# A decoder layer's last LayerNorm: square root on ScalarE with the reciprocal on VectorE, two and a half blocks scaled by TensorE, one store from ScalarE's queue

## The chip, the cores and the metric

The kernel runs on one core of one Trainium2 chip. The time is device microseconds of one execution; lower is better. The program is fully unrolled: there are no loops at run time, and each of the five engines (TensorE, VectorE, ScalarE, GpSimd, SyncE; PE, DVE, ACT, POOL, SP in the profile) works through its own list of instructions in order and waits on semaphores that the other engines and the transfers raise.

## The reference

One layer of a hybrid decoder on 256 tokens of width 2048 in float32: a feed-forward network (SwiGLU) with a residual and a LayerNorm, a mixer of sparse attention and a recurrent branch with its residual and LayerNorm, and a second SwiGLU with residual and LayerNorm. The change concerns only the last statement, and in it only what is done once the sums are there:

```python
def layer_norm(x, g, b):
    mu = jnp.mean(x, axis=-1, keepdims=True)
    var = jnp.mean(jnp.square(x - mu), axis=-1, keepdims=True)
    return (x - mu) * lax.rsqrt(var + LN_EPS) * g + b
...
h = layer_norm(DN_ALPHA * h + 0.5 * swiglu(h, ffn2_w_in, ffn2_w_out), ln3_g, ln3_b)
```

## The kernel before

All large products run on TensorE, float32 split into a high and a low part, so that a product is three matmuls (lines 732 to 734). The 256 tokens are two groups of 128, one token to a partition: t = 0 and t = 1. The 2048 columns are four blocks of 512: nb = 0 to 3. `Y[t][nb]` is a tile of 128 x 512 in SBUF that holds the residual, and in the end the output.

The end of the program is `out_product` of the second feed-forward network. `last_blocks` finishes the products in such an order that both blocks 2 and 3 of group 0 are done first, then block 2 of group 1, and last block 3 of group 1 in two halves of 256 columns (line 1064 adds a half to the residual, line 1065 takes its statistics; 877 and 878 do that for a whole block). Group 0 is normalised while TensorE still works on group 1. `OuterNorm.finish` then normalises group 1; nothing else is left to do in the program, so this is where it ends.

The norm of a group goes in these steps. `chain(t)` turns the statistics into mean and variance (`bn_aggr`, line 887), adds epsilon (888), and raises that to the power -1/2 on GpSimd (889); `self.mv[t]` is the mean and `self.r[t]` the reciprocal root. `first(t, nb)` is one VectorE instruction that subtracts the mean and multiplies by the gain row (996). `second(t, nb)` is another one that multiplies by `self.r[t]` and adds the bias row (1000), and after it `leave` issues the store of the block (1004).

For some blocks of group 1 the second step goes another way: TensorE has beforehand put the bias row into a PSUM tile, as identity times row (992); ScalarE makes a diagonal matrix `diag` out of the identity and `self.r[1]` (1011, tile `dg`); `by_pe` lets TensorE add `diag` times the block to the PSUM tile (1015), and ScalarE copies the result back to SBUF (1016). Before the change that is block 0 whole and block 1 in two halves of 256. Blocks 2 and 3 of group 1 go through VectorE, and VectorE takes the blocks in the order 2, 0, 1, 3.

A scheduler orders the instructions by the order of the code, with some pulled forward (`tc.high_priority()`). All nine stores are issued by SyncE, in the order in which `leave` is called. `SM`, `BP` and `U` hand out small tiles, PSUM tiles and 128 x 512 tiles; `T`, `V`, `A` and `G` are TensorE, VectorE, ScalarE and GpSimd; `S` is 256 and `P` 128.

Of the kernel before, what the change touches and what calls it, by code (L numbers as in the profile page):

```python
# [11 lines left out]
AF = mybir.ActivationFunctionType  # L12
# [3 lines left out]
P = 128  # L16
S = 256
# [11 lines left out]
EPS = 1e-5  # L29
# [331 lines left out]
def tile_layer(ctx, tc, x_fm, x_tm, pos, f1a, f1o, wA, wki, wB, wG, lru, wab, wrb, wo, f2a, f2o,  # L361
               cols_d, ln1_g, ln1_b, ln2_g, ln2_b, ln3_g, ln3_b, out):
    nc = tc.nc
# [4 lines left out]
    V, A, T, G = nc.vector, nc.scalar, nc.tensor, nc.gpsimd  # L368
    count = [0]

    def name(s):
        count[0] += 1
        return f"{s}{count[0]}"

    def U(s="u", dt=F32):
        return pool.tile([P, 512], dt, name=name(s), tag="u", bufs=U_BUFS)
# [7 lines left out]
    def SM(n, s="s", dt=F32):  # L384
        return pool.tile([P, 32], dt, name=name(s), tag="sm", bufs=21)[:, :n]

    def C(shape, s, dt=F32):
        return pool.tile(shape, dt, name=s)

    def MM():  # L390
        return psum.tile([P, 512], F32, name=name("mm"), tag="mm", bufs=4)

    def BP():
        return psum.tile([P, 512], F32, name=name("bp"), tag="bp", bufs=4)
# [60 lines left out]
    for i in range(NR + LAG):  # L455
# [4 lines left out]
        if i >= LAG:  # L460
            g, c = divmod(i - LAG, TPG)
            o = sum(LRU_COLS[:c])
# [62 lines left out]
        G.memset(invf[:, i:i + 1], float(THETA ** (-(2.0 * i) / 32)))  # L525
    mhalf = C([P, 1], "mhalf")
    G.memset(mhalf, -0.5)

    def col(k, i):
        o, w = COLS[k]  # L530
        return cols[:, o + i:o + i + 1]

    ident = C([P, P], "ident")
# [141 lines left out]
    Y = [[None] * 4 for _ in range(2)]  # L675

    sums = [[[spill.tile([P, 512], F32, name=name("ya")) for _ in range(4)] for _ in range(2)] for _ in range(2)]
# [149 lines left out]
    def blockA(x, finish=None, lag=0, ln=None):  # L827
# [18 lines left out]
        for k0, k1 in ranges:  # L846
            ws = []
            for k in range(k0, k1):
                ws.append(W.unit(512))
                half(0, k, ws[-1])  # L850
            if finish and k1 == n:
                finish(ps)
            for k in range(k0, k1):
                if ln and k == n - 2:
                    ln.half(0)
                half(1, k, ws[k - k0])
# [13 lines left out]
    stats = {}  # L870
# [95 lines left out]
    class OuterNorm(Norm):  # L966
# [17 lines left out]
        def finish(self):  # L984


            with tc.high_priority():
                self.chain(1)
            sums = {}
            for nb, o, w in ((0, 0, 512), (1, 0, S), (1, S, S)):  # L990
                ps = sums[nb, o] = BP()[:, :w]
                T.matmul(ps, ident, self.rows[1][nb][:, o:o + w], start=True, stop=False)

            def first(t, nb):
                y = Y[t][nb]
                V.scalar_tensor_tensor(y, y, self.mv[t], self.rows[0][nb], op0=OP.subtract, op1=OP.mult)

            def second(t, nb, o=0, w=512):
                y = Y[t][nb][:, o:o + w]
                V.scalar_tensor_tensor(y, y, self.r[t], self.rows[1][nb][:, o:o + w], op0=OP.mult, op1=OP.add)  # L1000
                leave(t, nb, o, w)

            def leave(t, nb, o=0, w=512):
                nc.sync.dma_start(out[t * P:(t + 1) * P, nb * 512 + o:nb * 512 + o + w], Y[t][nb][:, o:o + w])

            for nb in range(4):
                first(0, nb)
            for nb in range(4):
                second(0, nb)
            diag = U("dg")[:, :P]  # L1010
            A.activation(diag, ident, AF.Copy, scale=self.r[1])

            def by_pe(nb, o=0, w=512):
                ps, y = sums[nb, o], Y[1][nb][:, o:o + w]
                T.matmul(ps, diag, y, start=False, stop=True)
                A.activation(y, ps, AF.Copy)

            first(1, 2)
            first(1, 0)
            by_pe(0)  # L1020
            second(1, 2)
            leave(1, 0)
            first(1, 1)
            by_pe(1, 0, S)
            by_pe(1, S, S)
            first(1, 3)
            second(1, 3, 0, S)
            second(1, 3, S, S)
            leave(1, 1)

    def last_blocks(x, done):

# [172 lines left out]
    bias = C([P, 3 * P], "bias")  # L1205
# [305 lines left out]
    for j in range(-1, NR + LAG):  # L1511
# [15 lines left out]
        if j >= LAG:  # L1527
# [3 lines left out]
            if c == 1:  # L1531
                open_heads = [BP() for _ in range(4)]
                ws = [W.unit(P) for _ in range(2)]
                for m in range(2):
                    for wi_, xi in ((0, 0), (0, 1), (1, 0)):
                        for b in range(4):
                            rows = slice(b * TAIL, (b + 1) * TAIL)
                            T.matmul(open_heads[b][:, m * S:(m + 1) * S], ws[m][wi_][rows], xg[0][rows, xi],
                                     start=m == 0 and wi_ == 0 and xi == 0, stop=False)
            if c:  # L1540
                ps = open_heads[c - 1]
# [3 lines left out]
            if c == TPG - 1:  # L1545
                ps = MM()
# [134 lines left out]
```

## Time and profile before

| | us |
|---|---|
| runs | 2359.98, 2359.97, 2358.42 (median 2359.97) |
| the profiled execution | 2358.41 |
| its span, first to last instruction | 2356.6 |
| PE, DVE, ACT, POOL busy | 2342.8, 2204.0, 1564.7, 264.5 |
| last instruction of TensorE's main products starts at | 2346.24 |

The rest, from the last product to the end of the span, is about 10 us, and this is all that the change touches, but for one small instruction at the start of the program. Rows of the timeline give the start in us from the beginning of the span, the busy time, the engine, the line, the operation, the tile written and the tiles read, the shape, how many instructions are merged in the row, and in brackets the idle time of the engine ahead of it with what ended it. SPq is SyncE's own list of issued transfers. The time to landing of a transfer counts from the start of its issue.

### The profile page before, as it was taken

The numbers are of one execution on the slowest core, as the hardware profiler recorded it, in microseconds if no ns is written. First come the engines' busy times: TensorE is split into PE (matmuls) and PEld (weight loads), VectorE is DVE, ScalarE is ACT, GpSimd is POOL, SyncE is SP. The second block draws the span as 40 slices with busy tenths as digits, with TensorE's granted clock in tenths as the row PEclk, the third lists the DMA queues.
The fourth block names the chain that finished last, engine by engine and source line by source line (L and its number), as shares of the span: only waits on it lengthen the run. The fifth ranks groups of instructions, "written<-read, shape, count | busy, mean of one in ns | idle before, by whom it ended". The sixth has DMA issues, their size and how long they took to land.

```text
span 2356.6 us, 40517 instructions
## 1 busy us (share of the span) xinstructions
PE 2342.8 (99%) x15430; PEld 2120.5 (90%) x15430; DVE 2204.0 (94%) x3197; ACT 1564.7 (66%) x2271; POOL 264.5 (11%) x368
## 2 busy tenths in 40 slices
PE   9999999999999999999999999999999999999998
PEld 7899999999988999888899998888889999999997
DVE  7999999999999999879887778998999999999997
ACT  7677777777757656556557785545667777777763
POOL 1101111111110000000100001100011111111111
PEclk9999999999999999999999999999999999999999
DMA  9888898888876555554765558755788888888876
GB/s 333 249 240 241 252 264 244 255 249 255 242 217 233 188 189 199 181 198 137 249 238 184 198 171 319 241 197 176 236 280 237 251 252 251 241 258 263 242 220 213
DMA packets 142180, 546.99 MB, mean 232 GB/s; under 512 B 16640, under 2 KB 17280, under 8 KB 117536
## 3 DMA queue, kind: packets, MB, share of 16 engines
q1 hardware_dynamic: 100944, 455.13, 55.2%
q0 software_dynamic: 41040, 89.27, 18.5%
q8 instruction: 121, 1.98, 0.3%
q14 instruction: 75, 0.61, 0.1%
HBM read 507.10 MB, written 37.22 MB: 231 GB/s over the span
## 4 chain that ended last, share of the span: by engine, by line
PE 92%; DVE 4%; issue 2%; DMA 1%; ACT 0%; POOL 0%; SPq 0%; POOLq 0%; DVEq 0%; ACTq 0%
PE mm L732 19%; PE mm L733 19%; PE mm L734 19%; PE bp L733 7%; PE bp L734 7%; PE bp L732 7%; PE mm L1376 3%; PE mm L1375 3%; PE mm L1374 3%; DVE wl L269 2%; PE bp L1136 1%; ACT wh L268 0%; DMA raw<-f1a 0%; DMA x<-x_fm 0%; PE bp L1340 0%
## 5 line engine op out<-in xcount | busy, mean ns | idle before, releaser
L268 ACT ACTIVATE wh<-rf 128x1024 fp32r<-128x1024 f32 x573 | 512.0, 913 | 236.8 <-DVE rf L235 115.7
L269 DVE TENSOR_TENSOR wl<-rf,wh 128x1024 fp32r<-128x1024 f32 x573 | 596.1, 1045 | 11.4 <-ACT wh L268 7.6
L268 ACT ACTIVATE wh<-raw 128x1024 fp32r<-128x1024 f32 (+3 forms) x402 | 409.9, 1038 | 207.1 <-PE mm L734 94.2
L269 DVE TENSOR_TENSOR wl<-raw,wh 128x1024 fp32r<-128x1024 f32 (+3 forms) x402 | 473.9, 1196 | 71.1 <-ACT wh L268 68.6
L733 PE MATMUL bp<-wl,sh 128*128 128x256 f32 x1146 | 322.3, 281 | 1.0 <-DVE wl L269 0.9
L732 PE MATMUL bp<-wh,sh 128*128 128x256 f32 x1146 | 320.8, 280 | 0.0
L734 PE MATMUL bp<-wh,sl 128*128 128x256 f32 x1146 | 320.2, 279 | 0.0
L732 PE MATMUL mm<-wh,hs 128*128 128x512 f32 (+1 forms) x800 | 275.9, 345 | 0.8 <-DVE z L1124 0.5
L734 PE MATMUL mm<-wh,hs 128*128 128x512 f32 (+1 forms) x800 | 269.8, 337 | 0.1
L733 PE MATMUL mm<-wl,hs 128*128 128x512 f32 (+1 forms) x800 | 269.8, 337 | 0.0
L268 ACT ACTIVATE wh<-ws 128x1024 fp32r<-128x1024 f32 x191 | 202.0, 1058 | 92.0 <-DVE ws L228 58.1
L228 DVE TENSOR_TENSOR ws<-rf 128x1024 f32<-128x1024 f32 x191 | 233.6, 1223 | 5.0 <-DMA rf<-wrb 1.9
L269 DVE TENSOR_TENSOR wl<-ws,wh 128x1024 fp32r<-128x1024 f32 x191 | 233.9, 1225 | 3.3 <-ACT wh L268 3.2
L733 PEld LDWEIGHTS bp<-wl,sh 128*128 128x128 f32 x1146 | 215.4, 188 | 5.8 <-DVE wl L269 2.1
L732 PEld LDWEIGHTS bp<-wh,sh 128*128 128x128 f32 x1146 | 215.4, 188 | 1.5
L734 PEld LDWEIGHTS bp<-wh,sl 128*128 128x128 f32 x1146 | 215.4, 188 | 0.0
L1374 PE MATMUL mm<-hs,wh 128*128 128x256 f32 x640 | 180.3, 282 | 0.0
L1376 PE MATMUL mm<-hs,wl 128*128 128x256 f32 x640 | 179.8, 281 | 0.0
L1375 PE MATMUL mm<-hs,wh 128*128 128x256 f32 x640 | 179.8, 281 | 0.0
L732 PEld LDWEIGHTS mm<-wh,hs 128*128 128x128 f32 x800 | 150.3, 188 | 19.5 <-issue 2.2
L734 PEld LDWEIGHTS mm<-wh,hs 128*128 128x128 f32 x800 | 150.2, 188 | 18.7 <-DVE hs L926 0.5
L733 PEld LDWEIGHTS mm<-wl,hs 128*128 128x128 f32 x800 | 150.4, 188 | 16.2
(357 smaller groups left out, 5908.2 us busy)
## 6 DMA issues: line engine op xcount, KB each, us to landing
rf<-f1a SPq DMA_DIRECT2D x75, 1024.0 KB, 7.7
rf<-f2a SPq DMA_DIRECT2D x75, 1024.0 KB, 7.7
raw<-f1o SPq DMA_DIRECT2D x88, 512.0 KB, 6.6
raw<-f2o SPq DMA_DIRECT2D x88, 512.0 KB, 6.7
raw<-wB SPq DMA_DIRECT2D x80, 512.0 KB, 4.7
raw<-wG SPq DMA_DIRECT2D x54, 512.0 KB, 4.4
ya<-yd POOLq DMA_DIRECT2D x80, 256.0 KB, 8.1
rf<-wA SPq DMA_DIRECT2D x20, 1024.0 KB, 5.2
```

The source lines that it names most:

```text
L228: v.tensor_tensor(t, b[:, 0:4:3], b[:, 1:2].to_broadcast([P, 2, 2, 256]), op=OP.add)
L268: nc.scalar.activation(hp, src, AF.Copy)
L269: self.last = nc.vector.tensor_tensor(lp, src, hp, op=OP.subtract)
L732: T.matmul(ps, xh, w[0], start=start, stop=False)
L733: T.matmul(ps, xh, w[1], start=False, stop=False)
L734: T.matmul(ps, xl, w[0], start=False, stop=stop)
L1136: T.transpose(ps[:, k * S + t * P:k * S + (t + 1) * P], z[:, t * 512 + k * P:t * 512 + (k + 1) * P], ident)
L1374: T.matmul(ps[:, :S], w[0], x[:, 0], start=first, stop=False)
L1375: T.matmul(ps[:, :S], w[0], x[:, 1], start=False, stop=False)
L1376: T.matmul(ps[:, :S], w[1], x[:, 0], start=False, stop=last)
```

## The change

At the start GpSimd fills one more constant column, `eps` (one memset). The rest is in `finish`:

- The reciprocal root of group 1 is no longer made by VectorE (add) and GpSimd (power). ScalarE takes the square root of variance plus epsilon, with epsilon as the bias operand, and VectorE takes the reciprocal.
- VectorE takes all four `first` of group 1 in the order 0, 1, 2, 3, with the reciprocal behind the first of them.
- TensorE scales blocks 0 and 1 whole and the left half of block 2. VectorE's `second` does the right half of block 2 and then block 3 whole.
- The stores of group 1 go out in the order block 0, block 1, right half of block 2, block 3 on SyncE's queue. The left half of block 2 is stored from ScalarE's queue.
- `tc.manual_schedule()` keeps the instructions of this part in the order of the code.

```diff
--- before.py
+++ after.py
@@ -525,6 +525,8 @@
         G.memset(invf[:, i:i + 1], float(THETA ** (-(2.0 * i) / 32)))
     mhalf = C([P, 1], "mhalf")
     G.memset(mhalf, -0.5)
+    eps = C([P, 1], "eps")
+    G.memset(eps, EPS)
 
     def col(k, i):
         o, w = COLS[k]
@@ -984,12 +986,16 @@
         def finish(self):
 
 
+            mv, sd = SM(2), SM(1)
             with tc.high_priority():
-                self.chain(1)
+                V.bn_aggr(mv, stats["st"][1])
+                A.activation(sd, mv[:, 1:2], AF.Sqrt, bias=eps)
+            self.mv.append(mv[:, 0:1])
+            self.r.append(SM(1))
             sums = {}
-            for nb, o, w in ((0, 0, 512), (1, 0, S), (1, S, S)):
-                ps = sums[nb, o] = BP()[:, :w]
-                T.matmul(ps, ident, self.rows[1][nb][:, o:o + w], start=True, stop=False)
+            for nb, w in ((0, 512), (1, 512), (2, S)):
+                ps = sums[nb] = BP()[:, :w]
+                T.matmul(ps, ident, self.rows[1][nb][:, :w], start=True, stop=False)
 
             def first(t, nb):
                 y = Y[t][nb]
@@ -1000,33 +1006,33 @@
                 V.scalar_tensor_tensor(y, y, self.r[t], self.rows[1][nb][:, o:o + w], op0=OP.mult, op1=OP.add)
                 leave(t, nb, o, w)
 
-            def leave(t, nb, o=0, w=512):
-                nc.sync.dma_start(out[t * P:(t + 1) * P, nb * 512 + o:nb * 512 + o + w], Y[t][nb][:, o:o + w])
+            def leave(t, nb, o=0, w=512, queue=nc.sync):
+                queue.dma_start(out[t * P:(t + 1) * P, nb * 512 + o:nb * 512 + o + w], Y[t][nb][:, o:o + w])
 
             for nb in range(4):
                 first(0, nb)
             for nb in range(4):
                 second(0, nb)
             diag = U("dg")[:, :P]
-            A.activation(diag, ident, AF.Copy, scale=self.r[1])
-
-            def by_pe(nb, o=0, w=512):
-                ps, y = sums[nb, o], Y[1][nb][:, o:o + w]
-                T.matmul(ps, diag, y, start=False, stop=True)
-                A.activation(y, ps, AF.Copy)
-
-            first(1, 2)
-            first(1, 0)
-            by_pe(0)
-            second(1, 2)
-            leave(1, 0)
-            first(1, 1)
-            by_pe(1, 0, S)
-            by_pe(1, S, S)
-            first(1, 3)
-            second(1, 3, 0, S)
-            second(1, 3, S, S)
-            leave(1, 1)
+
+            def by_pe(nb, w=512, queue=nc.sync):
+                y = Y[1][nb][:, :w]
+                T.matmul(sums[nb], diag, y, start=False, stop=True)
+                A.activation(y, sums[nb], AF.Copy)
+                leave(1, nb, 0, w, queue)
+
+            with tc.manual_schedule():
+                first(1, 0)
+                V.reciprocal(self.r[1], sd)
+                A.activation(diag, ident, AF.Copy, scale=self.r[1])
+                by_pe(0)
+                first(1, 1)
+                by_pe(1)
+                first(1, 2)
+                by_pe(2, S, nc.scalar)
+                first(1, 3)
+                second(1, 2, S, S)
+                second(1, 3)
 
     def last_blocks(x, done):
```

Apart from these rows the order of every engine is unchanged. The rows below are the engines' own lists; the tiles y_26466, y_26506, y_26557 and y_26601 are blocks 0, 1, 2 and 3 of group 1 before, and y_26468, y_26508, y_26559 and y_26603 the same blocks after. Line numbers after are higher by 2 to 6.

VectorE, from the aggregate of group 1's statistics to the end of the program, before:

```order
L887 BN_AGGR s_26792<-st_26435 128x2
L888 TENSOR_SCALAR s_26793<-s_26792 128x1
L996 SCALAR_TENSOR_TENSOR y_26557<-y_26557,s_26792,row_26619 128x512
L996 SCALAR_TENSOR_TENSOR y_26466<-y_26466,s_26792,row_26619 128x512
L1000 SCALAR_TENSOR_TENSOR y_26557<-y_26557,s_26794,row_26623 128x512
L996 SCALAR_TENSOR_TENSOR y_26506<-y_26506,s_26792,row_26619 128x512
L996 SCALAR_TENSOR_TENSOR y_26601<-y_26601,s_26792,row_26619 128x512
L1000 SCALAR_TENSOR_TENSOR y_26601<-y_26601,s_26794,row_26623 128x256 x2
```

And after, in the same place:

```order
L991 BN_AGGR s_26794<-st_26437 128x2
L1002 SCALAR_TENSOR_TENSOR y_26468<-y_26468,s_26794,row_26621 128x512
L1026 RECIPROCAL s_26798<-s_26795 128x1
L1002 SCALAR_TENSOR_TENSOR y_26508<-y_26508,s_26794,row_26621 128x512
L1002 SCALAR_TENSOR_TENSOR y_26559<-y_26559,s_26794,row_26621 128x512
L1002 SCALAR_TENSOR_TENSOR y_26603<-y_26603,s_26794,row_26621 128x512
L1006 SCALAR_TENSOR_TENSOR y_26559<-y_26559,s_26798,row_26625 128x256
L1006 SCALAR_TENSOR_TENSOR y_26603<-y_26603,s_26798,row_26625 128x512
```

The whole `second` of block 2 has left the middle of the list, a half of it stands near the end, and the reciprocal is one place behind the aggregate's first user.

ScalarE, the end of its list before, with what each row waits for in brackets (`wd` is a high part of the last weights):

```order
L253 ACTIVATE wd_26670<-raw_26595 128x512
L1011 ACTIVATE dg_26816<-ident,s_26794 128x128 [waits Pool_49]
L1016 ACTIVATE y_26466<-bp_26798 128x512 [waits PE_49]
L1016 ACTIVATE y_26506<-bp_26800 128x256 [waits PE_49]
L1016 ACTIVATE y_26506<-bp_26802 128x256 [waits PE_49]
```

And after:

```order
L253 ACTIVATE wd_26672<-raw_26597 128x512
L992 ACT_TABLE_LOAD
L992 ACTIVATE s_26795<-s_26794,eps 128x1 [waits DVE_49]
L1027 ACTIVATE dg_26817<-ident,s_26798 128x128 [waits DVE_49]
L1021 ACTIVATE y_26468<-bp_26799 128x512 [waits PE_49]
L1021 ACTIVATE y_26508<-bp_26801 128x512 [waits PE_49]
L1021 ACTIVATE y_26559<-bp_26803 128x256 [waits PE_49]
L1010 DMA out<-y_26559 128x256 [waits Activation_49]
```

The list has a load of the activation tables more (the square root is in another table than the functions before it), the root, and a transfer at its end.

SyncE, the stores of group 1 before:

```order
L1004 DMA out<-y_26557 128x512 [waits DMAHW0_49,DVE_49]
L1004 DMA out<-y_26466 128x512 [waits DMAHW1_49,Activation_49]
L1004 DMA out<-y_26601 128x256 [waits DMAHW2_49,DVE_49]
L1004 DMA out<-y_26601 128x256 [waits DMAHW3_49,DVE_49]
L1004 DMA out<-y_26506 128x512 [waits DMAHW4_49,Activation_49]
```

And after:

```order
L1010 DMA out<-y_26468 128x512 [waits DMAHW0_49,Activation_49]
L1010 DMA out<-y_26508 128x512 [waits DMAHW1_49,Activation_49]
L1010 DMA out<-y_26559 128x256 [waits DMAHW3_49,DVE_49]
L1010 DMA out<-y_26603 128x512 [waits DMAHW4_49,DVE_49]
```

The first store of group 1 was one that waits for VectorE; now the first two wait for ScalarE's copies, and both stores of VectorE's blocks stand behind them.

## The prediction

> **What bounds the kernel now.** I read the page first, then the timeline of the last 10 us, the chain of waits there, SyncE's own waits, and the DMA traffic in short windows. The page:
>
> ```profile
> span 2356.6 us, 40517 instructions
> PE 2342.8 (99%) x15430; PEld 2120.5 (90%) x15430; DVE 2204.0 (94%) x3197; ACT 1564.7 (66%) x2271; POOL 264.5 (11%) x368
> ```
>
> TensorE sets the time nearly to the end, and the change leaves its list there as it is. What can move is the end, where TensorE has run out of products. The timeline of it, engine by engine:
>
> ```profile
> 2346.36 1.89 PE L992 MATMUL bp<-row,ident 128*128 128x512 f32 x6
> 2349.52 2.28 PE L1015 MATMUL bp<-y,dg 128*128 128x512 f32 x6 [1.27 <-ACT dg L1011]
> ...
> 2347.49 0.29 DVE L887 BATCH_NORM_AGGREGATE s<-st 128x2 f32<-128x30 f32 x1
> 2347.81 0.15 DVE L888 TENSOR_SCALAR s<-s 128x1 f32<-128x1 f32 x1
> 2347.88 1.41 DVE L996 SCALAR_TENSOR_TENSOR y<-y,s,row 128x512 f32<-128x512 f32 x2
> 2348.05 0.99 POOL L889 TENSOR_TENSOR s<-s,mhalf 128x1 f32<-128x1 f32 x1 [8.37 <-DVE s L888]
> 2349.07 0.40 ACT L1011 ACTIVATE dg<-ident,s 128x128 f32<-128x128 f32 x1 [19.49 <-POOL s L889]
> 2349.20 0.75 DVE L1000 SCALAR_TENSOR_TENSOR y<-y,s,row 128x512 f32<-128x512 f32 x1
> 2349.87 1.41 DVE L996 SCALAR_TENSOR_TENSOR y<-y,s,row 128x512 f32<-128x512 f32 x2
> 2350.68 1.54 ACT L1016 ACTIVATE y<-bp 128x512 f32<-128x512 f32 x3 [1.22 <-PE bp L1015]
> 2351.31 0.88 DVE L1000 SCALAR_TENSOR_TENSOR y<-y,s,row 128x256 f32<-128x256 f32 x2
> ```
>
> The mean and variance are ready at 2347.78; the power on GpSimd ends at 2349.04 and only then can the diagonal be made. The chain of waits says the same and gives TensorE's steps: 1.13 us from the diagonal to the copy of block 0 (512 columns), and 1.15 more for both halves of block 1:
>
> ```profile
> 2349.07 0.41 ACT dg L1011
> ...
> 2349.52 1.13 PE bp L1015 x2
> ...
> 2350.67 1.15 PE bp L1015 x4
> ```
>
> All arithmetic is over at 2352.22, yet the span ends at 2356.6. In between are the stores. Block 2 goes out at 2349.98 (the first of five, which the merged row gives), block 0 at 2351.3, then the three that follow, the last (block 1, 256 KB) at 2352.77. SyncE then waits for them to land, four times, 2.0 us:
>
> ```profile
> 2349.98 3.17 SPq L1004 DMA_DIRECT2D out<-y  x5
> ...
> L1004 SPq DMA_DIRECT2D out<-y x1: 332/332/332, 2351.3 to 2351.3; - x1
> ...
> 2351.82 0.83 SPq L1004 DMA_DIRECT2D out<-y  x2
> ...
> 2352.25 0.41 SPq L1004 DMA_DIRECT2D out<-y  x1
> ...
> 2352.77 0.38 SPq L1004 DMA_DIRECT2D out<-y  x1
> ...
> SPq L1677 <- DMA out<-y: 2.0, 4, 0.7
> ```
>
> The landing of the first store of group 1, which had the DMA engines to itself, took 2.3 us, that of the last 2.7:
>
> ```profile
> DMA to landing us min/median/max: 2.3/2.3/2.3
> DMA to landing us min/median/max: 2.7/2.7/2.7
> ```
>
> So the last store landed at 2352.77 + 2.7 = 2355.47, 0.4 us later than an unhindered one, and 1.1 us of closing steps follow. What hinders it is seen in the windows (DMA share and GB/s are the last two columns):
>
> ```profile
> 2350.50:2350.75 0.25, 0.23 (x2) 0.09 (x1) 0.25 (x2) 0.07 (x1) 0.00 (x0) 1.00 0.00 0
> 2350.75:2351.00 0.25, 0.25 (x2) 0.22 (x3) 0.25 (x1) 0.25 (x1) 0.00 (x0) 1.00 0.75 287
> ...
> 2353.00:2354.00 1.00, 0.00 (x0) 0.00 (x0) 0.00 (x0) 0.00 (x0) 0.00 (x0) 1.00 1.01 325
> 2354.00:2355.00 1.00, 0.00 (x0) 0.00 (x0) 0.00 (x0) 0.00 (x0) 0.00 (x0) 1.00 0.43 150
> ```
>
> Data of a store begin about 0.82 us after its issue (2349.98 to 2350.81, since the second window is three quarters full), and from 2353 to 2354 the 16 DMA engines are full at 325 GB/s. The last 768 KB (blocks 0, 3, 1; 786 thousand bytes) take 786/325 = 2.42 us: 2351.30 + 0.82 + 2.42 = 2354.54, which is where the windows run empty. The end is thus a stream of data that starts with block 0's store, rather than the last issue.
>
> **The root (gain).** Out go one VectorE add and the 0.99 us power on GpSimd. In come a root of 128x1 on ScalarE and a reciprocal of 128x1. No row has just this root. Near ones:
>
> ```profile
> L588 ACT ACTIVATE cs<-s 128x32 f32<-128x32 f32 x1 | 0.2, 221 | 0.0
> L1482 ACT ACTIVATE vw<-vw 128x256 f32<-128x256 f32 x20 | 6.6, 405 | 0.0
> L1353 DVE RECIPROCAL s<-s 128x2 f32<-128x2 f32 x16 | 2.6, 161 | 0.6 <-ACT s L1351 0.4
> ```
>
> L1482 is a root of 128x256. Between 0.22 and 0.41 us, then; the root starts at 2347.82 and ends by 2348.04 to 2348.23. VectorE meanwhile does `first` of block 0, 1.41/2 = 0.705 us from 2347.81, and reaches the reciprocal at about 2348.52, so either bound of the root is hidden. The wait that this adds on VectorE (reciprocal for ScalarE, three `first` queued behind it) costs nothing as long as the root takes under 0.7 us. Reciprocal to 2348.68, diagonal 2348.71 to 2349.11, TensorE from 2349.15 instead of 2349.52: 0.37 us sooner. TensorE is free by then: its bias products grow from 1024 to 1280 columns, 1.89 x 1.25 = 2.36, to 2348.72.
>
> The table load ahead of the root is 1.28 us. It has no wait of its own, and ScalarE has been idle 19.49 us there. That a load does not wait for its function's operand shows at the program's start, where it ran 1.9 us before the first input had landed:
>
> ```profile
> 0.74 1.28 ACT L507 ACT_TABLE_LOAD   x1 [0.74 <-PEq L1673]
> 3.89 0.72 ACT L507 ACTIVATE xs<-x 128x256 fp32r<-128x256 f32 x2 [1.86 <-DMA x<-x_fm]
> ```
>
> I take it as nothing. The Trainium skill speaks against the root here: "ScalarE: Activation LUTs", section What ACT_TABLE_LOAD costs, gives 1283 ns for the load and about 1380 ns for a drain, some 2.66 us for every change of set. The trace agrees on the 1283; by the rule's whole price, if it fell behind the aggregate, the time would be the table rival's below.
>
> **TensorE scales 1280 columns instead of 1024.** Block 0 is ready 1.13 us after the start, at 2350.28. For what each further 512 columns cost I have two bounds: 1.13 (the first block again) and 0.76 (1.89 for 1024 columns at L992 less the first 1.13). Nothing waits between the blocks, as VectorE has done `first` of block 1 by 2349.4, and L992 is the row without waits; I take 0.76. Block 1 is ready at 2351.04, the half of block 2 at 2351.42. ScalarE's copies by these rows (0.60 for 512 columns, 0.38 for 256) end at 2350.91, 2351.67 and 2352.06; with 1.13 the second ends at 2352.04.
>
> ```profile
> L1016 ACT ACTIVATE y<-bp 128x256 f32<-128x256 f32 x2 | 0.8, 384 | 0.2
> L1016 ACT ACTIVATE y<-bp 128x512 f32<-128x512 f32 x1 | 0.6, 597 | 1.2 <-PE bp L1015 1.2
> ```
>
> **VectorE.** Four `first` at 0.705, the reciprocal's 0.1, half a `second` of 0.44 and a whole one of 0.75, from 2347.81: done at 2351.92, against 2352.19 before. This gain is covered: block 3's store stands behind two others on SyncE.
>
> **The stores.** SyncE: block 0 at 2350.94, block 1 at 2351.70, right half of block 2 behind it (0.33 issue and 0.10 between two issues, as between 2351.82 and 2352.25) at 2352.13, block 3 at 2352.13 + 0.41 + 0.11 = 2352.65. That the right half is ready at 2351.2 is of no use; it is queued behind the wait for block 1's copy. ScalarE's queue issues the left half at about 2352.09. The last issue is 0.12 us sooner than before. But block 2, whose 256 KB went out at 2349.98 ahead of the rest, is now in the stream: 256 KB of block 0 move alone from 2351.76 to 2352.5, and 768 KB are left, starting with block 1's store: 2351.70 + 0.82 + 2.42 = 2354.94, against 2354.54. That is 0.40 us later. The second queue adds no engines: in the windows they are full already with one queue. The Trainium skill has this as a rule ("Trainium Kernel Development and Optimization", Key Constraints): transfers issued from different engines share the same 16 DMA engines, and several queues save only issue time. The trace agrees for one queue, at a share of 1.01; two at once are shown by no run yet.
>
> A store from ScalarE's queue is shown by no row. Its bounds are the landings of other stores (2.3 to 2.7 us) and those of the first transfers that the other two queues made in the program:
>
> ```profile
> x<-x_fm SPq DMA_DIRECT2D x8, 256.0 KB, 7.2
> posi<-pos POOLq DMA_DIRECT2D x1, 1.0 KB, 5.7
> ```
>
> The first of these were issued together with many loads, so I take the near rows, 2.7.
>
> **GpSimd's new constant** costs what its neighbour does, 0.09 us, at 3.3 us into the program. GpSimd's first transfer behind it carries the residual, not the operands that TensorE starts with, so it is hidden; bare, it is 0.09.
>
> ```profile
> 3.33 0.09 POOL L527 MEMSET mhalf<- 128x1 f32 x1
> ```
>
> **Sum.** Root -0.37, which the moved stream of stores more than takes back: the end of the data, which already has the root in it, goes from 2354.54 to 2354.94, +0.40. Bounds: -0.12, if the last issue decides rather than the data, and +0.77, if a further 512 columns cost 1.13 (block 1's store then at 2352.07). Against the profiled execution's 2358.41 us (2356.6 span and 1.8 around it) that is 2358.8. This execution equals the fastest run shown (2358.42); the median, 2359.97, is 1.56 us above it, so I forecast 2359.97 + 0.40 = 2360.4, own range 2359.8 to 2360.7 on the median, 2358.3 to 2359.1 on the fastest. The measurement tells about 0.2%, 4.7 us, from no change: this is no change.
>
> **Rivals.** *The root's gain comes through.* If the end hangs on the arithmetic, the 0.37 us stay: 2359.6. For it: the sooner last issue. Against it: full DMA engines, and one store of 2.7 us where 2.3 was possible.
>
> *The table load is not covered.* If it runs only once the root's operand is there, the root ends at 2347.82 + 1.28 + 0.28 = 2349.38 (0.28 lies between the root's bounds), and the reciprocal holds up VectorE and the diagonal by 2349.42 - 2348.52 = 0.90: 2361.3. With the 2.66 us of the skill's page it would be 2362.7. Against it: the rows at 0.74 and 3.89.
>
> *ScalarE's queue is slow on its first use* (the other side). If its store lands only after 7.2 us as SyncE's first ones did, it does so at 2352.09 + 7.2 = 2359.3, 3.8 us after the old end: 2363.8. It decides from a landing of about 3.8 us on (2352.09 + 3.8 = 2355.87, the forecast's last landing), and passes 0.2% at 8.1. For it: the queue carries nothing else in the program. Against it: it has no load traffic beside it, as those first transfers had.
>
> **How the numbers follow.** Forecast 0.62, gain comes through 0.16, table load bare 0.08, slow queue 0.09, something else 0.05. The single times lie within 1.6 us of each other for reasons that none of these cases touch, so the range reaches below the gain's 2359.6 by that spread, to 2357.8, and above the table rival with the page's price, to 2363.0; left out are the slow queue and most of the unnamed. Faster by over 0.2% would need 2355.2, which no case gives: 0.02. Slower by over 0.2% is half of the slow queue: 0.05. The rest, 0.93, is the same.
>
> **What the changed profile would show.** The table load between 2329.6 and 2347.8, not behind the aggregate; the root under 0.7 us with VectorE not idle ahead of the reciprocal; the diagonal at about 2348.7; TensorE's six scaling matmuls without a gap, over at 2351.4; SyncE's last issue near 2352.65 and landings of 3 us or so; DMA windows full from 2352.5 to 2354.9. Wrong would be: a reciprocal that waits, a store on ScalarE's queue that lands last by far, or a stalled issue. One such stall stands in the trace, among the stores of group 0, 1.53 us against a median of 0.34:
>
> ```profile
> L1004 SPq DMA_DIRECT2D out<-y x9: 332/344/1530, 2342.5 to 2352.8; - x9
> ```

## The result and the profile after

The changed kernel takes 2344.59 us (2343.40 to 2346.82, six runs) against 2359.97 us (2358.42 to 2362.33, six runs): a ratio of 0.9937, 95% interval 0.9926 to 0.9947. That is 15 us faster, where no measurable change was forecast and the range reached down only to 2357.8. The profiled execution took 2343.40 us. One of the ten runs of experiment 5 below took 9508.05 us and is left out of its ratio.

The page of the changed kernel, its first lines and the shares of the chain that ended last:

```profile
span 2341.6 us, 40516 instructions
...
PE 2324.1 (99%) x15430; PEld 2113.4 (90%) x15430; DVE 2201.3 (94%) x3196; ACT 1562.2 (67%) x2273; POOL 263.5 (11%) x368
...
PE 49%; DVE 37%; issue 8%; DMA 2%; ACT 2%; POOL 0%; SPq 0%; ACTq 0%; DVEq 0%; POOLq 0%
```

The same last line of the page before:

```profile
PE 92%; DVE 4%; issue 2%; DMA 1%; ACT 0%; POOL 0%; SPq 0%; POOLq 0%; DVEq 0%; ACTq 0%
```

TensorE has the same 15430 matmuls and is busy 18.7 us less. The chain, which ran over TensorE almost alone, now runs over VectorE for 37%. So the time seems to have been saved among the products, whose instructions the change doesn't touch. The granted clock is no part of it: it is 1.00 in both profiles. First the end, which the change does touch. The timeline of it, after the change (the main products' last matmul stands first):

```profile
2330.94 0.28 PE L736 MATMUL bp<-wd,g 128*128 128x256 f32 x1
2331.06 2.31 PE L998 MATMUL bp<-row,ident 128*128 128x512 f32 x6
2333.82 2.42 PE L1020 MATMUL bp<-y,dg 128*128 128x512 f32 x6 [0.45 <-ACT dg L1027]
...
2314.47 1.28 ACT L992 ACT_TABLE_LOAD   x1
2332.50 0.29 ACT L992 ACTIVATE s<-s,eps 128x1 f32<-128x1 f32 x1 [16.76 <-DVE s L991]
2333.36 0.40 ACT L1027 ACTIVATE dg<-ident,s 128x128 f32<-128x128 f32 x1 [0.56 <-DVE s L1026]
2334.98 0.60 ACT L1021 ACTIVATE y<-bp 128x512 f32<-128x512 f32 x1 [1.22 <-PE bp L1020]
2335.84 0.87 ACT L1021 ACTIVATE y<-bp 128x512 f32<-128x512 f32 x2 [0.26 <-PE bp L1020]
2336.74 0.41 ACTq L1010 DMA_DIRECT2D out<-y  x1
...
2333.17 0.16 DVE L1026 RECIPROCAL s<-s 128x1 f32<-128x1 f32 x1
...
2337.38 0.40 SPq L1010 DMA_DIRECT2D out<-y  x1
```

From the start of that matmul to the end of the span are 2341.6 - 2330.94 = 10.66 us, against 2356.6 - 2346.24 = 10.36 before. The end has become longer by 0.3 us (0.37 by the unrounded records), not shorter.

So 15.3 us are gone ahead of the end. Two lines of code, each with the start of its first and its last instruction, tell where. First the statistics on VectorE, then one of the recurrent branch's products on TensorE, before the change:

```profile
L878 DVE BATCH_NORM_STATS2 st<-y x23: 675/689/695, 683.9 to 2342.4; 128x6 f32<-128x512 f32 x23
...
L1375 PE MATMUL mm<-hs,wh x640: 277/280/285, 761.9 to 1392.9; 128*128 128x256 f32 x160
```

And after:

```profile
L880 DVE BATCH_NORM_STATS2 st<-y x23: 673/684/695, 684.2 to 2327.2; 128x6 f32<-128x512 f32 x23
...
L1381 PE MATMUL mm<-hs,wh x640: 276/276/286, 762.1 to 1382.4; 128*128 128x256 f32 x160
```

Up to 684 us, where the first feed-forward network ends, nothing has been gained. Between the first and the last instruction of L1375, 631.0 us have become 620.3: 10.7 us are saved, and these are the same instructions in the same order. The median duration of that matmul went from 280 to 276 ns. The groups of TensorE's work by shape show it again, before (columns behind the bar: busy us, mean ns of one, idle us ahead):

```profile
L734 PE MATMUL mm<-wd,g 128*128 128x512 f32 x292 | 113.6, 389 | 0.0
...
L1375 PE MATMUL mm<-hs,wh 128*128 128x256 f32 x640 | 179.8, 281 | 0.0
...
L733 PE MATMUL mm<-wl,ya 128*128 128x512 f32 x80 | 31.6, 395 | 0.0
```

and after:

```profile
L1381 PE MATMUL mm<-hs,wh 128*128 128x256 f32 x640 | 177.0, 277 | 0.0
...
L735 PE MATMUL mm<-wl,ya 128*128 128x512 f32 x80 | 31.1, 389 | 0.0
```

The page before held the hint: one shape, 128x512, takes 389 ns in one group and 395 in another, without a wait in either. The start of the next matmul comes earlier than a row's mean says (medians from the starts in the traces): 389 stands for 227 ns from start to start, 395 for 234, 277 for 113 and 281 for 117.

What can make the same matmul shorter? Ahead of the end the built programs differ in `eps` alone: one more memset, and the place that it takes. `eps`, 4 bytes in each partition, takes 32 bytes of SBUF and stands among the first constants. So the change reaches further than the end and one small instruction: all tiles behind `eps` lie 32 bytes further on, the high and low weight parts `wh` and `wl` among them (their address in bytes, modulo 256, goes from 160 to 192), and `z`, `rf`, `ws`. The 128 x 512 tiles (`hs`, `sh`, `g`, `ya`, `wd`) stand ahead of it and stay at 128.

A matmul reads two operands from SBUF: the moving one, which a row names first, and the stationary one, which is loaded ahead of it (PEld in the page); `T.matmul` takes them the other way round. Either can be a part of the model's weights: `wl` is the moving operand of `mm<-wl,ya` and `wh` the stationary one of `mm<-hs,wh`.

### The profile page after: what moved, and what is told of

The parts are those of the page before. It is cut to its first block, busy times and chain, and to the rows that moved or that the text cites. A ratio compares the mean times of both kernels' runs of the same rounds, so it can differ in the third digit from the quotient of the medians.

```text
span 2341.6 us, 40516 instructions
## 1 busy us (share of the span) xinstructions
PE 2324.1 (99%) x15430; PEld 2113.4 (90%) x15430; DVE 2201.3 (94%) x3196; ACT 1562.2 (67%) x2273; POOL 263.5 (11%) x368
## 4 chain that ended last, share of the span: by engine, by line
PE 49%; DVE 37%; issue 8%; DMA 2%; ACT 2%; POOL 0%; SPq 0%; ACTq 0%; DVEq 0%; POOLq 0%
DVE wl L269 20%; PE mm L734 10%; PE mm L736 10%; PE mm L735 10%; DVE ws L228 5%; DVE rf L235 3%; PE mm L1381 3%; DVE rf L232 3%; PE mm L1380 3%; PE mm L1382 3%; PE bp L735 3%; PE bp L736 3%; PE bp L734 3%; ACT wh L268 2%; DVE z L1130 1%
## 5 line engine op out<-in xcount | busy, mean ns | idle before, releaser
L1380 PE MATMUL mm<-hs,wh 128*128 128x256 f32 x640 | 177.6, 278 | 0.0
L1381 PE MATMUL mm<-hs,wh 128*128 128x256 f32 x640 | 177.0, 277 | 0.0
```

What stands on the lines that cost most here:

```text
L1380: T.matmul(ps[:, :S], w[0], x[:, 0], start=first, stop=False)
L1381: T.matmul(ps[:, :S], w[0], x[:, 1], start=False, stop=False)
```

## The experiments

Experiments 1, 3 to 7 and 9 are the kernel before with some tiles moved in SBUF and no instruction changed; 2, 10 and 11 start from the changed kernel; 8 and 12 leave the layer out. Ratios are to the kernel before, run again beside each group of experiments (medians 2359.1 to 2359.8 us).

### 1. Before, with everything behind `mhalf` 32 bytes further

```diff
-    mhalf = C([P, 1], "mhalf")
+    mhalf = C([P, 16], "mhalf")[:, :1]
```

> The kernel before with one edit: the tile of mhalf is 64 bytes a partition wide instead of 4 (rounded up to 32), so every tile behind it lies 32 bytes higher, as after the change. No instruction is added, removed or moved. Theory A (address): the tiles wh and wl come to lie on multiples of 64 bytes and the matmuls that read them take less; all of the gain but the tail's +0.3 us: 2344.3 us, ratio 0.9935, and the 512-wide matmuls on wl with a median distance of 226 ns instead of 234. Theory B (the new end of the norm makes the gain): 2360 us, ratio 1.000. Theory C (the additional instruction at the start shifts the timing of everything): 2360 us, since there is none here.

2343.74 us, ratio 0.9934 (0.9917 to 0.9950). The whole gain is there with the old norm, old stores and the power on GpSimd. Its groups read as those of the changed kernel:

```profile
L1375 PE MATMUL mm<-hs,wh 128*128 128x256 f32 x640 | 177.1, 277 | 0.0
...
L733 PE MATMUL mm<-wl,ya 128*128 128x512 f32 x80 | 31.2, 389 | 0.0
```

### 2. After, with `eps` in the second column of `mhalf`'s tile

```diff
-    mhalf = C([P, 1], "mhalf")
+    half = C([P, 2], "mhalf")
+    mhalf, eps = half[:, 0:1], half[:, 1:2]
...
-    eps = C([P, 1], "eps")
```

> The changed kernel, whole, but epsilon lies in a second column of the tile of mhalf, so that no other tile moves. Theory A: the gain is gone, and the end of the norm costs what its stage shows: 2360.3 us, ratio 1.000, last product to end of span 10.6 to 10.8 us against 10.36 before. Theory B: 2344.6 us, ratio 0.9935. Theory C: 2344.6 us, since the additional instruction is here.

2360.35 us, ratio 1.0003 (0.9993 to 1.0012), with the old durations:

```profile
L1381 PE MATMUL mm<-hs,wh 128*128 128x256 f32 x640 | 179.8, 281 | 0.0
...
L735 PE MATMUL mm<-wl,ya 128*128 128x512 f32 x80 | 31.6, 395 | 0.0
```

The change in the norm and the stores, all of it but the address, is worth nothing that can be measured.

### 3. 64 bytes further

```diff
-    mhalf = C([P, 1], "mhalf")
+    mhalf = C([P, 24], "mhalf")[:, :1]
```

> The kernel before with the tile of mhalf 96 bytes wide: everything behind it lies 64 bytes higher, wh and wl again 32 bytes past a multiple of 64. Theory A, as alignment to 64 bytes: as before, 2360 us, ratio 1.000, median distance 234 ns. Theory A', as any other distance between the tiles that happens to fall better: 2344 to 2350 us.

2375.90 us, ratio 1.0072 (1.0057 to 1.0087): 16 us slower than before, which neither theory had. The feed-forward's 256-wide product, 280 ns before, is what got longer here, along with the 512-wide one:

```profile
L732 PE MATMUL bp<-wh,sh 128*128 128x256 f32 x1146 | 324.8, 283 | 0.0
...
L733 PE MATMUL mm<-wl,ya 128*128 128x512 f32 x80 | 31.9, 399 | 0.0
```

### 4. 32 bytes less

```diff
-    posi = C([P, 2], "posi", I32)
+    small = C([P, 8], "small")
+    posi, mhalf = small[:, :2].bitcast(I32), small[:, 4:5]
...
-    mhalf = C([P, 1], "mhalf")
```

> The kernel before with mhalf moved into the unused part of the tile of posi: everything behind it lies 32 bytes lower, wh and wl on multiples of 64 (and of 128). Theory A, alignment to 64: 2344.3 us, ratio 0.9935, median distance 226 ns. Theory A' (a higher position is better): 2360 us or more. If multiples of 128 count too, below 2342 us.

2360.89 us, ratio 1.0004 (0.9994 to 1.0013). The 512-wide product is faster and the 256-wide ones slower, which cancels:

```profile
L1375 PE MATMUL mm<-hs,wh 128*128 128x256 f32 x640 | 181.2, 283 | 0.0
...
L733 PE MATMUL mm<-wl,ya 128*128 128x512 f32 x80 | 31.3, 391 | 0.0
```

`wh` and `wl` lie on a multiple of 128 bytes here, and on one of 64 in experiment 1. So with 3 this rules out that a round boundary by itself is what the tiles want.

### 5. and 6. Only the weights, or only the tiles of the other engines

Experiment 4 with one tile between the two sorts made 32 bytes longer: `wh` and `wl` 32 bytes less, `z`, `rf` and `ws` as before.

```diff
-    kiT = C([P, S], "kiT")
+    kiT = C([P, S + 8], "kiT")[:, :S]
```

> The kernel before with wh and wl 32 bytes lower (as in the run with everything 32 lower, ratio 1.0004) and z, rf, ws, yd and the 256-wide tiles behind them where they were. Theory M (only the tiles that TensorE reads matter): as that run, 2360.9 us, ratio 1.000, distances 227 ns for 512 columns and 120 ns for 256. Theory V (VectorE's and ScalarE's tiles z, rf, ws matter as well): off by more than 3 us.

2361.10 us, ratio 1.0007 (0.9997 to 1.0017), with 283 and 391 ns as in 4:

```profile
L1375 PE MATMUL mm<-hs,wh 128*128 128x256 f32 x640 | 181.4, 283 | 0.0
```

Then the widened `kiT` alone, the rest of the kernel as before: `wh` and `wl` as before, the tiles behind them 32 bytes further.

> The kernel before with wh and wl unmoved and z, rf, ws, yd and the 256-wide tiles behind them 32 bytes higher. Theory M: 2359.8 us, ratio 1.000, matmul distances as before (234 and 117 ns). Theory V: towards 2344 us, at least 3 us faster.

2359.62 us, ratio 1.0000 (0.9991 to 1.0009), with 281 and 396 ns:

```profile
L733 PE MATMUL mm<-wl,ya 128*128 128x512 f32 x80 | 31.6, 396 | 0.0
```

Moving the tiles that ScalarE, VectorE and the DMAs alone read and write by 32 bytes changes nothing that can be measured; of the tiles moved here, only TensorE's operands count.

### 7. 96 bytes less

```diff
-    posi = C([P, 2], "posi", I32)
+    small = C([P, 64], "small")
+    posi, mhalf = small[:, :2].bitcast(I32), small[:, 2:3]
...
-    hba = C([P, NR], "hba")
-    hbx = C([P, NR], "hbx")
-    sp2 = C([P, NR], "sp2")
+    hba, hbx, sp2 = (small[:, 4 + i * NR:4 + (i + 1) * NR] for i in range(3))
```

Modulo 128 this is the place of experiment 1, modulo 256 it isn't.

> The kernel before with posi, mhalf, hba, hbx and sp2 in one tile of 256 bytes, so that everything behind lies 96 bytes lower: wh and wl come to the same place in 128 bytes (64) as with 32 bytes higher, but to another in 256 (64 instead of 192). Seen so far: 32 lower 1.0004, unmoved 1, 32 higher 0.9934, 64 higher 1.0072. Theory P128 (the place within 128 bytes decides): 2343.7 us, ratio 0.9934, 256-wide matmuls on hs with wh as weights at 113 ns. Theory P256 or longer: anything else, say 2360 us. Theory D (other things move with the instructions on the small tiles): 2360 us with matmul distances as before.

2353.44 us, ratio 0.9975 (0.9966 to 0.9985): 6 us faster, between the two, so that the place modulo 128 does not decide. In this kernel TensorE waits for the weights' low parts, which VectorE makes, and the chain turns to VectorE:

```profile
L731 PE MATMUL bp<-wl,sh 128*128 128x256 f32 x1146 | 322.3, 281 | 9.0 <-DVE wl L269 9.0
...
PE 58%; DVE 27%; issue 9%; DMA 3%; ACT 2%; POOL 1%; SPq 0%; POOLq 0%; DVEq 0%; ACTq 0%
```

### 8. TensorE alone

A kernel without the layer: 64 groups of 48 matmuls, 512 and 256 columns, eight moving tiles 32 bytes apart (modulo 256) against four stationary tiles 32 bytes apart, no other engine at work beside it.

```python
for w in (512, 256):
    for s in STA:                       # sa 96, sb 128, sc 160, sd 192 modulo 256
        for m in MOV:                   # ma 128, mb 160, ... me 0, ... mh 96
            for j in range(48):
                T.matmul(ps, s[:, j % 2 * P:...], m[:, j // 2 % 2 * 512:...], ...)
```

> Leaves the whole layer out: after one load and twelve copies it runs 64 groups of 48 matmuls of 128x512 or 128x256 with 128x128 weights that change with every matmul, while no other engine or transfer works. The moving tile lies at 0, 32, ... 224 bytes past a multiple of 256 (ma at 128, mb 160, mc 192, md 224, me 0, mf 32, mg 64, mh 96), the weights at 96, 128, 160 and 192 (sa, sb, sc, sd). Theory P (TensorE's own two reads of SBUF, the moving one and that of the next weights, hinder each other by their places): with weights at 128 (sb), 512 columns take 227 ns with the moving tile at 128, 234 at 160, 226 to 231 at 192 and 231 to 238 at 224, and 256 columns differ by up to 7 ns between the places. Theory W (the other engines' and the transfers' traffic on the same memory makes the difference): all groups of one width within 1 ns of each other.

The distance is the address of the moving operand less that of the stationary one, modulo 256. At 512 columns one distance has one time, whatever the two places are (the very first group, in which TensorE starts up, left aside):

```profile
L42 PE MATMUL acc<-md,sb 128*128 128x512 f32 x48 | 11.4, 395 | 0.0
...
L42 PE MATMUL acc<-mb,sb 128*128 128x512 f32 x48 | 11.4, 395 | 0.0
...
L42 PE MATMUL acc<-mc,sb 128*128 128x512 f32 x48 | 11.2, 392 | 0.0
L42 PE MATMUL acc<-me,sd 128*128 128x512 f32 x48 | 11.2, 392 | 0.0
L42 PE MATMUL acc<-ma,sb 128*128 128x512 f32 x48 | 11.1, 389 | 0.0
L42 PE MATMUL acc<-mc,sd 128*128 128x512 f32 x48 | 11.1, 389 | 0.0
```

Distance 0 gives 389, distance 64 gives 392, the others 394 to 396. Since no other engine works here, other traffic isn't needed for it.

### 9. Both moved: the distance of 1 at the place of 3

```diff
+    mhalf = C([P, 1], "mhalf")          # ahead of the 128 x 512 tiles
...
-    invf = C([P, 16], "invf")
+    invf = C([P, 32], "invf")[:, :16]
...
-    mhalf = C([P, 1], "mhalf")
```

`wh` and `wl` stand 64 bytes further, as in 3, and the 128 x 512 tiles 32 bytes further, so that the distance between them is that of 1.

> The kernel before with the 128x512 tiles (x, hs, g, y and the like, which hold TensorE's other operand, and wd) 32 bytes higher and wh and wl 64 bytes higher. Theory R (the distance of the two operands of a matmul within 256 bytes decides): wh and wl are 64 bytes past the other operand, as with everything behind mhalf 32 higher: 2343.7 us, ratio 0.9934, 229 to 231 ns for 512 columns, 113 ns for hs with wh in the recurrent branch. Theory P (wh's and wl's own place decides): they lie where they lay in the run with 64 higher, so 2376 us, ratio 1.007.

2344.52 us, ratio 0.9936 (0.9919 to 0.9952), where the same place of `wh` and `wl` gave 2375.90 in 3. Distance, not place:

```profile
L1375 PE MATMUL mm<-hs,wh 128*128 128x256 f32 x640 | 177.2, 277 | 0.0
...
L733 PE MATMUL mm<-wl,ya 128*128 128x512 f32 x80 | 31.2, 389 | 0.0
```

### 10. After, with the left half of block 2 stored by SyncE

```diff
-                by_pe(2, S, nc.scalar)
+                by_pe(2, S)
```

> The changed kernel with the left half of block 2 stored from SyncE's queue too, ahead of the right half. From the start of the last main matmul to the end of the span the changed kernel takes 10.66 us. Theory S (the stream of the last 768 KB decides, and a second queue adds nothing): 10.6 to 10.8. Theory I (the last issue decides): SyncE's last issue comes 0.5 us later, 11.1.

A single run, 2345.88 us; only its end is compared. Its last main matmul and last issue:

```profile
2332.65 0.28 PE L736 MATMUL bp<-wd,g 128*128 128x256 f32 x1
...
2339.62 0.38 SPq L1010 DMA_DIRECT2D out<-y  x1
```

Its span is 2343.3, so the end is 10.65 us, as after (10.66), though the last issue comes 6.97 us behind that matmul instead of 6.44. The data end 8.65 us behind that matmul (8.64 after). In this pair of executions the second queue makes the last issue sooner and saves no time.

### 11. After, with the old root (VectorE's add, GpSimd's power)

```diff
-                A.activation(sd, mv[:, 1:2], AF.Sqrt, bias=eps)
+                V.tensor_scalar(sd, mv[:, 1:2], EPS, None, op0=OP.add)
+                r = SM(1)
+                G.tensor_tensor(r, sd, mhalf, op=OP.pow)
...
-                V.reciprocal(self.r[1], sd)
```

> The changed kernel with the old root of group 1: VectorE adds epsilon, GpSimd raises to -1/2; everything else as changed, and the addresses too. If the new root is worth what the prediction says, 0.37 us on the path to the stores, the end takes 11.0 instead of 10.66 us. If the root lies beside other work, 10.7.

The last main matmul and the diagonal:

```profile
2331.03 0.28 PE L736 MATMUL bp<-wd,g 128*128 128x256 f32 x1
...
2333.85 0.40 ACT L1028 ACTIVATE dg<-ident,s 128x128 f32<-128x128 f32 x1 [19.30 <-POOL s L994]
```

A single run, 2344.12 us, span 2342.2. The diagonal starts 2.82 us behind the last matmul (after: 2.42) and the end is 11.17 us long (after: 10.66). The new root is thus worth 0.4 us up to the diagonal and 0.4 to 0.5 at the end of the span (0.44 by the unrounded records), in one execution of each.

### 12. TensorE alone, 256 columns, repeated

As 8, with the stationary tiles at 0: each of the eight distances in four other orders and with two patterns of stationary tiles.

```python
T.matmul(ps, (s, s, u)[j % 3][:, j // 3 % 2 * P:...], x[:, (0, 256, 0)[j % 3]:...], ...)   # L43; s, u are sf, sg
T.matmul(ps, sj[:, j % 2 * P:...], x[:, j // 2 % 2 * 512:...], ...)                       # L46, as in 8
```

> Leaves the layer out: groups of 48 matmuls of 256 columns alone on the core, with the moving tile at eight places in 256 bytes, each in four repeats (pa to pd) in another order, and in two patterns: weights from two halves of one tile in turn (sj), or as the recurrent branch has them, twice from one tile and once from another (sf, sf, sg), all weights at place 0. Theory R: the time of a matmul is a function of the distance and the pattern, within 1 ns in all repeats; the recurrent branch's pattern with the moving tile 64 below the weights (mc at 192) takes 113 ns and with 64 above (mg at 64) 118. Theory L (the pair of reads can fall into one of several rhythms, by what came before): at one distance some repeats take 113 and others 118.

`me`, `mg` and `mc` stand at distances 0, 64 and 192:

```profile
L43 PE MATMUL pa<-me,sf 128*128 128x256 f32 x32 | 5.8, 283 | 0.0
...
L43 PE MATMUL pa<-mg,sf 128*128 128x256 f32 x32 | 5.7, 280 | 0.0
...
L46 PE MATMUL pa<-mc,sj 128*128 128x256 f32 x48 | 5.6, 277 | 0.0
L46 PE MATMUL pb<-mc,sj 128*128 128x256 f32 x48 | 5.6, 277 | 0.0
```

All eight groups of a distance agree to within 1.4 ns from start to start (the first group of the run left aside); 192 bytes gave 113.3 to 113.9.

## Why the prediction was wrong, and where it was right

The step that failed is the one on GpSimd's new constant. It priced `eps` as a memset of 0.09 us, hidden, and didn't ask where the constant lies. Its cost was not the memset but the place: 32 bytes that move `wh` and `wl` against the 128 x 512 tiles, worth 15.3 us ahead of the end. Neither the terms of the sum nor any rival named addresses, and "TensorE sets the time nearly to the end, and the change leaves its list there as it is" was true of the list and not of the time of its items.

How the 15 us follow from the distance is seen by setting the runs beside the two kernels of TensorE alone. Times are in ns from one start to the next, worked out from the starts of the matmuls in the traces: means of the groups alone, and medians of the large groups (60 matmuls or more) in the layer's kernels.

| distance | 512 wide, alone (exp. 8) | 512 wide in the layer, `wh` or `wl` moving | 256 wide, alone (exp. 8, 12) | 256 wide in the layer |
|---|---|---|---|---|
| 0 | 227 | 227 (exp. 4) | 120 | 120 (exp. 4) |
| 32 | 233 | 233 to 234 (before) | 117 to 118 | 116 to 117 (before) |
| 64 | 229 | 226 to 232 (after) | 118, one group 113 | 118 (after); 117 to 118 (exp. 7, `hs` moving) |
| 96 | 234 | 231 to 238 (exp. 3) | 120 | 118 to 123 (exp. 3) |
| 128 | 233 | | 118 to 119 | |
| 160 | 234 | | 117 to 119 | 117 (exp. 3, `hs` moving) |
| 192 | 233 | 231 to 235 (exp. 7) | 118 (exp. 8), 113 to 114 (exp. 12) | 113 to 114 (after, `hs` moving); 114 to 117 (exp. 7) |
| 224 | 233 | | 118 | 117 (before, `hs` moving) |

Before, `wh` and `wl` lay 32 bytes behind the other operand's tile. Where they stream through TensorE 512 wide (attention, output products), the distance was 32 and is 64 now: 234 to some 229 ns. Where `hs` or `xc` streams 256 wide past them (the recurrent branch above all), it was 224 and is 192: 117 to 113. Both traces hold the same 15430 matmuls in the same order, so that each can be set beside itself. Over those that start between 640 and 1720 us before, the second kind went from 259.7 to 250.5 us from start to start and the first from 512.5 to 506.8. These 14.9 us are slightly more than the 14.4 us by which that part of the program became shorter. The rest, up to the last product, gained 1.1: in the feed-forward networks what the 512-wide matmuls gained the 256-wide ones nearly lost again, at 118 ns instead of 116 to 117. Experiment 3 is the converse: there many 256-wide matmuls went to 119 and more, and the two networks took 13.6 us more.

The rest, step by step:

- The new root, forecast at 0.37 us up to the diagonal, is worth 0.4 (experiment 11). It took 0.29 us, under VectorE's `first`, and the reciprocal did not wait. The diagonal came at 2333.36, which is 2348.66 on the clock of before (15.30 us later), against a forecast of 2348.71.
- The table load ran at 2314.47, 18 us ahead of its root, and cost nothing. By the Trainium skill ("ScalarE: Activation LUTs", What ACT_TABLE_LOAD costs) a drain of about 1380 ns belongs to it; the load's 1.28 us agrees, and a drain was nowhere on the path, since ScalarE had been idle for 16.76 us.
- TensorE's further blocks cost more than the 0.76 us taken: block 0 is copied from 2334.98 and block 1 from 2335.84, 0.86 apart, inside the two bounds.
- The stream of stores decides the end, as forecast, and takes the root's gain back. The changed kernel and experiments 2 and 10 take 10.69 to 10.71 us from the last product to the end, the eight kernels with the old end 10.29 to 10.57 (unrounded). The windows (DMA share and GB/s last) are full, but for two at 0.63 and 0.77 between the data of block 0 and those of block 1, and then run empty, here after the change:

```profile
2336.50:2336.75 0.25, 0.00 (x0) 0.00 (x0) 0.00 (x0) 0.21 (x1) 0.00 (x0) 1.00 1.00 385
...
2338.00:2339.00 1.00, 0.00 (x0) 0.00 (x0) 0.00 (x0) 0.00 (x0) 0.00 (x0) 1.00 1.01 346
...
2339.50:2339.75 0.25, 0.00 (x0) 0.00 (x0) 0.00 (x0) 0.00 (x0) 0.00 (x0) 1.00 0.30 98
2339.75:2340.00 0.25, 0.00 (x0) 0.00 (x0) 0.00 (x0) 0.00 (x0) 0.00 (x0) 1.00 0.01 0
```

  The data end at 2339.50 + 0.30 x 0.25 = 2339.58, or 2354.88 on the clock of before, against a forecast of 2354.94 and 2354.54 before: +0.34 where +0.40 stood in the sum. Two small errors cancel in this: block 1's store was issued at 2336.46 (2351.76; forecast 2351.70), and the last 768 KB took 2339.58 - 2336.46 - 0.82 = 2.30 us instead of 2.42. The last issue at 2337.38 (2352.68; forecast 2352.65) is sooner than before by 0.1 us and did not count.
- ScalarE's queue is not slow on its first use. Its transfer landed in 2.9 us (KB and us to landing last), so that rival falls:

```profile
out<-y SPq DMA_DIRECT2D x3, 256.0 KB, 2.4
out<-y ACTq DMA_DIRECT2D x1, 128.0 KB, 2.9
```

- That the second queue adds no engines was argued; experiment 10 agrees, since without that queue the end is as long. The rule that the prediction cited from the Trainium skill ("Trainium Kernel Development and Optimization", Key Constraints) now has a run with two queues beside one with a single queue: 10.66 and 10.65 us.

The sum for what the change was forecast to do holds: experiment 2, the change without the move, gives 2360.35 us against the forecast 2360.4. That they agree to 0.05 us is luck, since the interval of its ratio is 4.5 us wide; what bears the forecast out is the end, 0.37 us longer where 0.40 stood.

## What to carry to other kernels

Whoever adds or resizes a tile, however small, can move what is allocated behind it, and this kernel, bound by TensorE, gained or lost 16 us in 2360 by that alone; so compare the mean duration of equal matmuls before and after before crediting the edit, and run the edit once with the addresses held. If equal shapes differ by a few ns on one page without a wait (389 and 395 here), the distance between the moving and the stationary operand is a thing to try: constants padded by 32 bytes at a time are a cheap test. Which distance is best depends on the mix of widths: 0 was for 512 columns, and at 256 columns 192 gave the shortest times, though not in every run.

## What the runs showed of the hardware that was not expected

- The pace of equal float32 matmuls depends on the distance of their two SBUF operands modulo 256 bytes: 227 to 234 ns at 512 columns, 113 to 120 at 256. Tiles moved by +32, -96, -32 and +64 bytes gave kernels of 2343.74, 2353.44, 2360.89 and 2375.90 us.
- The Trainium skill ("SBUF — State Buffer", Who interferes with whom) has TensorE's reads of the moving operand and of the weights on two independent ports. Read that way, all distances would have one time; the runs of TensorE alone differ by up to 6%, and the measurement decides. Why the distance counts is shown by no run.
- Open: the distance doesn't settle everything at 256 columns. At 192 bytes experiment 12 had 113 ns in all groups and experiment 8 118; at 64 bytes one group of experiment 8 had 113 and the others 118. The places don't explain it: `ma` and `sd` of experiment 8 (128 and 192) stand where `hs` and `wh` stand after the change, and take 118, not 113. The layer shows several times at one distance too (experiment 7, at 192). Neither does it settle everything at 512 columns in the layer: `wd` is at distance 0 in all these kernels, and before, one of its three lines takes 389 ns and the others 393 and 394. Twelve of these matmuls from 523.4 us on take 234, 240, 229, ... 232, 231, 227 ns from start to start; in experiment 4, where the matmuls around them are at distance 0 as well, the same twelve reach 226 to 227 after six. So what came before seems to count as well; that was not tested by itself. Nor was it tried to give `wh` and `wl` unequal distances.
- A faster TensorE soon meets VectorE. In experiment 7 most of the feed-forward's 256-wide matmuls ran at 114 ns instead of 117, and the networks took almost as long as before (1.2 us less): TensorE then waited for VectorE's low parts, 9.0 us in the row of experiment 7 where the same row before has 0.9. The changed kernel, with 37% of its chain on VectorE and 1.5 us of this wait, seems to be on the way there. None of the kernels run is measurably faster than the changed one; experiment 1 equals it.
